# A RetNet and HGRN2 mixer step on one core: two spreads by TensorE go through DRAM, W_v sums move into the ramp, x sums move to VectorE, and some thirty positions in a hand-written order change

## The chip, the cores and the metric

The kernel runs on one core of one Trainium2 chip. The metric is device time in microseconds (us), the median of three runs of the whole program. Engine names are those of the profile: PE is TensorE, DVE is VectorE, ACT is ScalarE, POOL is GpSimd, SP is SyncE (which here only issues DMA).

## What is computed

One layer of a hybrid decoder, in fp32, for a prompt of 2048 tokens and for 8 new tokens ("decode rows") with their own states:

```python
h = rmsnorm(x, norm_g)
p = h @ w_in                              # 1024 -> 8 groups of 512
rq, rk, rv, rg, hq, hf, hi, hgate = split(p, 8)
o_ret, s_ret = chunked_decay_recurrence(rotary(rq), rotary(rk) * dk**-0.5, rv, log_gamma, s0)
o_hg,  s_hg  = chunked_decay_recurrence(silu(hq), (1 - lb) * sigmoid(-hf), hi, logf, s0)
o = concat(head_rmsnorm(o_ret) * silu(rg), head_rmsnorm(o_hg) * silu(hgate))
y = rmsnorm(x + o @ w_out, final_norm_g)
```

`rmsnorm` divides each token by its root mean square ("1/rms" below). Outputs are y for both sets of tokens and four new states.

## The kernel before

**Products.** Each fp32 operand is split into a high and a low part (ACT makes the high part, DVE subtracts it, L233, L272, L713), and a product is three matmuls, high by high, high by low, low by high. Big products are done in 2 x 2 blocks with seven block products in place of eight (Strassen-Winograd); the operands are sums of blocks, called T1 to T4 on one side and S1 to S4 on the other, beside plain blocks (A11, A12, A22, B11, B21, B22).

**Stages.** A *ramp* computes the values (retention and HGRN) of the first two token groups with plain products `pv` (L465), while loads come in; it begins with small warm-up matmuls `wu` (L200, L203) and holds the decode rows' value product `pvd` (L556). Then come units u = -6 to -1, the values of the other six groups; u = 0 to 23, the projections, three to a head group, with the HGRN steps in units 0, 3, 6, ... and the retention steps in units 2, 5, 8, ...; u = 24 to 31, the output projection. Each unit is seven slots long; a slot is one block product, twelve matmuls of 128 x 512 (`aV`, `eG`, `bR` and so on, L872).

**Order.** PE's program order is written out. For the other engines too the order is fixed: `at(pos, f)` puts a step on a heap at a position in slots (unit u starts at 7u; the values' units lie at negative positions), and steps are emitted by position. Most positions come from the table `AT`. Each engine runs its instructions strictly in that order, so that an instruction that waits holds up all behind it. SBUF tiles come from small rings: twelve temporary buffers, handed on in first-in, first-out order (`t_get`, `t_done`, L251, L267), and a few rings of named tiles. A DMA into a buffer waits for the buffer's last reader.

**The pieces that the change touches:**

- *x1's block rows.* x1 are the operands of the second half of the prompt. Its blocks are normalised by `x1_norm` (L1349), which multiplies by a row of 1/rms, laid along the free axis and the same on all partitions. To make it, `x1_dg` (L1314) puts four columns of 1/rms on the diagonals of four 128 x 128 blocks on DVE, `x1_spread` (L1321) multiplies ones by these on PE (`prb`, L701), copies the result on ACT and stores it to `rb_dram` on POOL's queue; `x1_rb` (L1343) loads it eight times on SP.
- *The decode row of 1/rms.* `decode_dg` (L578) and `decode_spread` (L581) do the same for the eight decode rows (`dgd`, `prsd`, `rbd`), and DVE then scales the decode tokens into `xz` (L586).
- *The W_v operands in the ramp.* `wv_subs` (L509) forms T1 to T4 of the value weights on DVE in place, `wv_parts` (L516) splits them, per k (0 to 3, each with k + 4). Those of k = 2, 3 end in the first unit (u = -6, position -42).
- *x sums.* `blocks_sums` (L424, operations L434) forms T1, T2, T3, T4 of the token blocks for the groups 6 and 7, in two halves each; two of these four are on DVE and two on POOL. Results are stored to `x_dram`; the next load waits for such stores.
- *Decode products.* `dec_mm` (L770, `pdp`, L778) multiplies the rows of W_in of a unit by `xz` on PE; for u = 3, 6, 9 it stands at `mm0`. It reads the freshly loaded weight blocks (`r3A`, `r3S`, loaded by `w_load`, L737).
- *Weight splits* (`w_split`, L757, ops L271 on ACT and L272 on DVE) make S1, S2, A12 and so on of the next unit's weights; *operand swaps* replace a low and high part of x1 or W_out (L709, L713); *rotation* `qr` (L967, L968, L716); *scores* `par` (L1140) and `pah`, `plh` (L1223, L1241, L1275, L1284), with the HGRN steps `kh`, `qth` (L1188, L1191) ahead of them; *transposes* `potr`, `poth` of the gated outputs and their gating `gtr`, `gth` (L1101, L1103).

Of the kernel before, what the change touches and what calls it, by code (L numbers as in the profile page):

```python
# [19 lines left out]
P = 128  # L20
# [28 lines left out]
def spooled(u):  # L49
# [10 lines left out]
          'load': 18.0,  # L60
# [10 lines left out]
 'ret': {'load': 12.0,  # L71
# [4 lines left out]
         'o0': 15.5,  # L76
         'st1': 15.7,
         'o1': 17.1,
         'last': 17.6,
         't0': 19.01,  # L80
         't1': 21.7},
# [6 lines left out]
       'sS1': -1.4,  # L88
# [3 lines left out]
       'sA12': 1.4,  # L92
       'sS3': 2.4,
       'sA22': 3.05},
 're': {'A11': -3.4, 'S1': -2.4, 'S2': -1.4, 'S4': -0.4, 'A12': 0.6, 'S3': 1.6, 'A22': 2.6},
 'dec': {'mm': -1.97, 'mm0': -3.42, 'copy': -0.9, 'copy0': -2.4, 'sel': 0.7},
# [10 lines left out]
          'B22': (8.9, 8.95, 9.2, 9.75),  # L107
          'B21': (9.45, 9.85, 10.0, 10.3),
          'T3': (11.3, 11.3, 11.8, 11.8),
          'T4': (14.2, 14.2, 14.7, 14.7)},  # L110
# [4 lines left out]
           'lB21': 6.4,  # L115
           'lT3': 8.4,
           'lT4': 12.2,
           'B11': (3.0, 3.0, 3.5, 3.5),
# [3 lines left out]
           'B21': (9.45, 9.85, 10.0, 10.3),  # L122
# [21 lines left out]
 'dhs': (-5.0, -2.2, -2.2, -1.5)}  # L144
# [5 lines left out]
def step_kernel(ctx, tc, a, out):  # L150
# [22 lines left out]
    vd_dram = dr.tile([2, NB, GW], F32, tag="vd_dram", name="vd_dram")  # L173
    v_dram = [
# [172 lines left out]

    spread_to = {}

# [74 lines left out]
    def blocks_sums(i, n):  # L424
# [8 lines left out]
        def less(o, x, y):  # L433
            (dve if (i, n) in ((6, 0), (7, 1)) else pool).tensor_tensor(o, x, y, op=ALU.subtract)  # L434
# [35 lines left out]
    def tok_load0(i, k0, cuts=1):  # L470
        r = x0r[i, k0] = t_get([P, 2, 256], f"x0r{i}{k0}")
        for n in range(0, 2, 2 // cuts):
            kk = slice(n, n + 2 // cuts)
            sp.dma_start(r[:, kk], a["x_t"][V_ORDER[i], :, k0 + kk.start : k0 + kk.stop])
# [101 lines left out]
    dgd = vq.tile([NB, NB], F32, tag="dgd", name="dgd")  # L576

    def decode_dg():  # L578
        dve.tensor_scalar(dgd, ident[:NB, :NB], rsd[:, 1:2], None, op0=ALU.mult)

    def decode_spread():  # L581
        pt = ps_tr.tile([P, NB], F32, tag="tr", name="prsd")
        pe.matmul(pt, ones[:NB, :], dgd, start=True, stop=True)
        rb = vq.tile([P, NB], F32, tag="rbd", name="rbd")
        act.activation(rb, pt, AF.Copy)
        dve.tensor_tensor(  # L586
            xz[:, : 32 * KT].rearrange("p (k b) -> p k b", b=32)[:, :, :NB], xs,
            rb.unsqueeze(1).to_broadcast([P, KT, NB]), op=ALU.mult,
        )
# [11 lines left out]
    tok_load0(0, 0, 2)  # L601
    wv_load(0, 2)
    act.activation(lb[:, 0:1], zero, AF.Sigmoid)
    tok_load0(0, 4)
    wv_load(4, 2)
    for k in (0, 4):
        x_split0(0, k)
        wv_split(k)
    wv_load(1)
    wv_load(5)  # L610
    for k in (1, 5):
        x_split0(0, k)
        wv_split(k)
    tok_load0(0, 2)
# [12 lines left out]
    sp.dma_start(pk, a["pack"])  # L627
    stats(1)
    decode_inputs()
    for k in range(KT):  # L630
        x_split0(1, k)
    pv0 = {(c, ty): bank([P, GW], f"pv0{c}{ty}") for c in range(2) for ty in range(2)}
# [5 lines left out]
    for m, k in enumerate((0, 4, 1, 5, 2, 6, 3, 7)):  # L638
        decode_values(m, k)
    first, second = ("T1", "T2"), ("T3", "T4")  # L640
# [9 lines left out]
    with tc.manual_schedule(engines=ORDERED):  # L650
        stats_load(2)
        for c in range(2):
            for ty in range(2):
                plain_out(0, c, ty, pv0[c, ty])
        wv_subs(0, first + second)
        wv_parts(0, first + second)
        tok_load(2)
        ps = plain_next(0, 1)
        stats_sum(2, True)
        stats_load(3)  # L660
        wv_subs(1, first + second)
        wv_parts(1, first + second)
        tok_load(3)
        plain_out(1, 0, 1, ps)
        stats_sum(3, True)
        spread_dg(2)
# [4 lines left out]
        wv_subs(2, first[:1])  # L671
        wv_subs(3, first[:1])
# [4 lines left out]
        wv_parts(2, first[:1])  # L677
        wv_parts(3, first[:1])
        tok_norm(2, 1)
        tok_sums(2, 0)  # L680
        s_split(2, "S1")
        plain_out(1, 0, 0, ps)
        wv_subs(2, second[:1])
        wv_subs(3, second[:1])
        wv_subs(2, first[1:])
# [1231 lines left out]
```

## Time and profile before

| | us |
|---|---|
| median of 3 runs (lowest, highest) | 1006.27 (1005.38, 1006.46) |
| the profiled execution | 1006.96 |
| its span, first to last instruction | 1005.2 |
| busy: PE, PE weight load | 987.3, 822.0 |
| busy: DVE, ACT, POOL | 783.6, 574.6, 256.2 |
| bytes moved | 244.56 MB, 243 GB/s |

Busy times are sums of instruction durations with overlaps counted once. Matmuls are pipelined: a 128 x 512 matmul lasts 0.39 us in a row, but the next starts 0.23 us after it, so that what a matmul costs is read from the difference of starts. DVE's operations overlap a little as well. A timeline row gives start, duration, engine, line of the kernel, operation, out<-in, the shape, and behind it in brackets the idle time before it with what ended it. Rows of a source line give shortest, median and longest duration in nanoseconds and the first and last start. A waits row gives total, count and longest wait. "issue" is time in which an engine waited for nothing that the profile shows.

### The profile page before, as it was taken

What the parts mean: (1) busy time and instruction counts of PE and PEld (TensorE: products, weight loads), DVE (VectorE), ACT (ScalarE), POOL (GpSimd) and SP (SyncE); (2) the same over time, 40 slices, a digit from 0 to 9 for tenths busy, and PEclk for the clock granted to TensorE, in tenths of its full rate; (3) what the DMA queues carried; (4) which work ended last, traced back from release to release, by engine and by line L of the source; (5) the groups of instructions that cost most, each with busy time, mean ns of one, the idle gap of its engine ahead of it and who ended that gap; (6) DMA issues with size and microseconds to landing.
All of it is one profiled execution on the core that took longest, in us unless ns stands there. A gap on an engine that the chain in (4) does not pass through costs nothing.

```text
span 1005.2 us, 22979 instructions
## 1 busy us (share of the span) xinstructions
PE 987.3 (98%) x8824; PEld 822.0 (82%) x8824; DVE 783.6 (78%) x1361; ACT 574.6 (57%) x1348; POOL 256.2 (25%) x404
## 2 busy tenths in 40 slices
PE   9999999999999999999999999999999999999997
PEld 8788877888888888888788788888888878877885
DVE  6797696879869978887898766877866799767774
ACT  7754523847655664765885555456467577524332
POOL 0211271112332433232012222222222602313121
PEclk9999999999999999999999999999999999999999
DMA  9746659838958878785985993993996396674522
GB/s 332 242 150 238 222 189 357 313 114 298 305 171 306 304 239 287 279 253 184 348 261 175 303 321 119 304 335 109 309 370 218 111 406 228 238 263 155 206 88 83
DMA packets 121340, 244.56 MB, mean 243 GB/s; under 512 B 12128, under 2 KB 52448, under 8 KB 118544
## 3 DMA queue, kind: packets, MB, share of 16 engines
q1 hardware_dynamic: 97968, 164.68, 48.9%
q0 software_dynamic: 22976, 78.17, 21.0%
q8 instruction: 69, 1.13, 0.5%
q14 instruction: 39, 0.32, 0.1%
q10 hardware_dynamic: 288, 0.27, 0.1%
HBM read 155.97 MB, written 90.24 MB: 245 GB/s over the span
## 4 chain that ended last, share of the span: by engine, by line
PE 84%; DVE 7%; ACT 4%; issue 2%; DMA 1%; POOL 1%; POOLq 0%; SPq 0%; DVEq 0%; ACTq 0%
PE aH L872 9%; PE aG L872 8%; PE aO L872 7%; PE aR L872 7%; PE aV L872 5%; PE eG L872 4%; PE eH L872 4%; PE pv L465 4%; PE eO L872 4%; PE eR L872 3%; PE eV L872 2%; PE bH L872 2%; PE bG L872 2%; PE bO L872 2%; PE bR L872 2%
## 5 line engine op out<-in xcount | busy, mean ns | idle before, releaser
L1639 ACT ACTIVATE yj<-xro 128x512 f32<-128x512 f32 x24 | 15.2, 632 | 66.9 <-DVE xro L716 33.2
L1202 ACT ACTIVATE qh<-kh 128x1024 f32<-128x1024 f32 x24 | 25.5, 1061 | 47.3 <-DVE kh L1188 47.3
L1188 DVE TENSOR_TENSOR kh<-kh,fph 128x512 f32<-128x512 f32 x48 | 32.9, 686 | 11.4 <-PE plh L1223 10.5
L949 ACT ACTIVATE sg<-g 128x512 f32<-128x512 f32 x26 | 16.4, 631 | 36.3 <-DVE g L716 35.8
L1082 ACT ACTIVATE obh<-poh 128x128 f32<-128x128 f32 x64 | 16.9, 287 | 32.5 <-PE poh L1078 32.5
L1191 DVE TENSOR_TENSOR qth<-qth,fph 128x512 f32<-128x512 f32 x48 | 32.9, 685 | 0.0
L1082 ACT ACTIVATE obr<-por 128x128 f32<-128x128 f32 x64 | 16.8, 276 | 27.3 <-PE por L1078 27.3
L716 DVE TENSOR_TENSOR xro<-aO,xro 128x512 f32<-128x512 f32 x33 | 22.5, 685 | 8.1 <-PE aO L872 7.8
L1106 POOL DMA_DIRECT2D o_dram<-gth x16 | 12.4, 773 | 62.6 <-DVE gth L1103 23.4
L1090 ACT ACTIVATE obh<-poh,orsh 128x128 f32<-128x128 f32 x64 | 18.2, 366 | 16.5 <-POOL orsh L229 16.4
L336 POOL TENSOR_TENSOR ms<-ms 128x2 f32<-128x2 f32 x8 | 3.0, 370 | 95.4 <-ACT xn L332 95.4
L956 POOL DMA_DIRECT2D g_dram<-g x31 | 16.9, 548 | 39.0 <-DVE g L952 33.9
L1090 ACT ACTIVATE obr<-por,orsr 128x128 f32<-128x128 f32 x64 | 18.2, 368 | 14.6 <-POOL orsr L229 14.6
L228 POOL TENSOR_SCALAR orsh<-omsh 128x4 f32<-128x4 f32 x16 | 4.9, 308 | 84.1 <-ACT obh L1082 83.8
L902 ACT ACTIVATE vo<-aV 128x512 f32<-128x512 f32 x12 | 7.1, 592 | 32.4 <-PE aV L872 32.1
L1069 DVE SCALAR_TENSOR_TENSOR sth<-sth,fph,puh 128x128 f32<-128x128 f32 x48 | 16.7, 347 | 11.0 <-PE poh L1078 8.5
L1106 POOL DMA_DIRECT2D o_dram<-gtr x16 | 12.5, 782 | 46.3 <-DVE g L716 14.0
L1076 PE MATMUL poh<-vh,A 128*128 128x128 f32 x128 | 24.0, 274 | 0.0
L1076 PE MATMUL por<-vr,A 128*128 128x128 f32 x128 | 24.0, 274 | 0.0
L228 POOL TENSOR_SCALAR orsr<-omsr,pk 128x4 f32<-128x4 f32 x16 | 7.6, 474 | 57.5 <-ACT obr L1082 57.5
L1653 DVE SCALAR_TENSOR_TENSOR xro<-xro,yms,fg 128x1024 f32<-128x1024 f32 (+1 forms) x16 | 19.9, 1245 | 3.0 <-POOL yms L1650 3.0
L1078 PE MATMUL poh<-sth,qth 128*128 128x128 f32 x112 | 21.7, 275 | 0.0
(1712 smaller groups left out, 3760.0 us busy)
## 6 DMA issues: line engine op xcount, KB each, us to landing
xn<-in_x_prompt SPq DMA_DIRECT2D x32, 256.0 KB, 4.7
v_dram<-vo SPq DMA_DIRECT2D x32, 256.0 KB, 3.4
xro<-in_x_prompt SPq DMA_DIRECT2D x16, 512.0 KB, 5.8
g_dram<-g POOLq DMA_DIRECT2D x31, 256.0 KB, 5.6
out_y_prompt<-xro POOLq DMA_DIRECT2D x15, 512.0 KB, 3.4
xr<-in_x_t SPq DMA_DIRECT2D x12, 512.0 KB, 5.7
vh<-v_dram SPq DMA_DIRECT2D x16, 256.0 KB, 8.0
gth<-g_dram SPq DMA_DIRECT2D x16, 256.0 KB, 6.8
```

Of the source, the lines that this page charges most:

```text
L465: pe.matmul(ps, xx, ww, start=(first and n == 0), stop=(last and n == 2))
L716: dve.tensor_tensor(o, x, y, op=ALU.add)
L872: pe.matmul(ps, w[i], x[j], start=(first and k == 0 and m == 0), stop=(k == 3 and m == 2), skip_group_check=True,)
L1076: pe.matmul(po[:, j], s_ctx["A"][:, c], box["v"][g][:, j], start=True, stop=src is None)
L1078: pe.matmul(po[:, j], qcol(c), src, start=False, stop=True)
L1082: act.activation(ob[:, j], po[:, j], AF.Square, accum_out=ms[:, j : j + 1])
L1090: act.activation(ob[:, j], po[:, j], AF.Copy, scale=rs[:, j : j + 1])
L1106: after(AT["gate"]["tr"], lambda: pool.dma_start(o_dram[c0 : c0 + 4, ty, :, h].rearrange("c p t -> p c t"), gt.rearrange("p (c t) -> p c t ...
L1188: dve.tensor_tensor(kv[:, :, 0, :], kv[:, :, 0, :], two[:, :, 1:2].to_broadcast([P, nb, b]), op=ALU.mult)
L1191: dve.tensor_tensor(qv[:, :, 1, :], qv[:, :, 1, :], two[:, :, 0:1].to_broadcast([P, nb, b]), op=ALU.mult)
L1202: act.activation(kept_k, k, AF.Copy)
L1653: dve.scalar_tensor_tensor(x[:, cc], x[:, cc], ms[:, 0:1], fg[:, cc], op0=ALU.mult, op1=ALU.mult)
```

## The change

1. *x1's block rows* leave PE. `x1_dg`, `x1_spread`, `blk_spread` and `rb_dram` are gone. `rows_store` stores four columns of 1/rms to `rs_dram` from POOL's queue, at positions -24.2 and -20.2, and `x1_rb` loads from it with a broadcast over partitions.
2. *The decode row* goes the same way: `decode_dg` is a store to `rsd_dram` on POOL's queue at -31.4, `decode_load` a broadcast load on SP at -24.4; the multiplication into `xz` stays at -15.4.
3. *Ramp.* The first x loads are cut into halves, and the decode tokens' part of `pack` is loaded first. The decode value product for k = 0, 4, 1, 5 stands in the middle of the first group's products, and the W_v sums and parts of k = 0, 1 behind it; those of k = 2, 3, and three steps of group 2, move from the first unit into the ramp. Warm-up: 25 pairs in place of 17.
4. *x sums* all run on DVE.
5. *Positions.* Some thirty entries of `AT` move, by 0.15 to 1.5 slots; u > 20 gets tables of its own for the retention and HGRN steps (`retL`, `hgrnL`), and u = 3 gets two HGRN steps half a slot earlier.

The diff, cut to its core:

```diff
- 'ret': {'load': 12.0,
+ 'ret': {'load': 12.5,
...
-          'o0': 15.5,
+          'o0': 15.0,
...
-          't0': 19.01,
-          't1': 21.7},
+          't0': 19.51,
+          't1': 23.2},
...
-       'sS1': -1.4,
+       'sS1': -1.25,
...
-       'sA12': 1.4,
-       'sS3': 2.4,
-       'sA22': 3.05},
+       'sA12': 1.9,
+       'sS3': 2.25,
+       'sA22': 3.3},
...
- 'dec': {'mm': -1.97, 'mm0': -3.42, 'copy': -0.9, 'copy0': -2.4, 'sel': 0.7},
+ 'dec': {'mm': -1.97, 'mm0': -3.92, 'copy': -0.9, 'copy0': -2.4, 'sel': 0.7},
...
- 'wu': 17,
- 'wop': (140.0, 1.8, 2.0, 2.6),
+ 'wu': 25,
+ 'wop': (140.0, 2.133, 2.1, 2.6),
...
- 'fin': 0.75,
+ 'fin': 1.0,
...
+    def rows_store(c):
+        pool.dma_start(rs_dram[c : c + 4].rearrange("c p -> p c"), rs_all[:, c : c + 4])
...
-            (dve if (i, n) in ((6, 0), (7, 1)) else pool).tensor_tensor(o, x, y, op=ALU.subtract)
+            dve.tensor_tensor(o, x, y, op=ALU.subtract)
...
     def decode_dg():
-        dve.tensor_scalar(dgd, ident[:NB, :NB], rsd[:, 1:2], None, op0=ALU.mult)
-
-    def decode_spread():
-        pt = ps_tr.tile([P, NB], F32, tag="tr", name="prsd")
-        pe.matmul(pt, ones[:NB, :], dgd, start=True, stop=True)
-        rb = vq.tile([P, NB], F32, tag="rbd", name="rbd")
-        act.activation(rb, pt, AF.Copy)
+        pool.dma_start(rsd_dram, rsd[:, 1:2])
+
+    def decode_load():
+        rbd = vq.tile([P, NB], F32, tag="rbd", name="rbd")
+        sp.dma_start(rbd, rsd_dram.partition_broadcast(P))
+        return rbd
...
+        if kk == 1:
+            decode_inputs()
+            for m, k in enumerate((0, 4, 1, 5)):
+                decode_values(m, k)
+            for k in range(2):
+                wv_subs(k, first + second)
+                wv_parts(k, first + second)
+    for m, k in enumerate((2, 6, 3, 7)):
+        decode_values(m + 4, k)
...
-    def blk_spread(blk, dg, dst):
-        pt = ps_tr.tile([P, 4, P], F32, tag="tr", name=f"prb{blk}")
-        for j in range(4):
-            pe.matmul(pt[:, j], ones, dg[:, j], start=True, stop=True)
-        act.activation(dst, pt.rearrange("p a b -> p (a b)"), AF.Copy)
...
-        sp.dma_start(xd["rb"], rb_dram[n])
+        c = 8 + 4 * TB[n]
+        sp.dma_start(xd["rb"].rearrange("p (c t) -> p c t", c=4), rs_dram[c : c + 4].partition_broadcast(P))
...
-    at(-21 + 3.6, decode_dg)
-    at(-21 + 5.6, decode_spread)
+
+    at(-35 + 3.6, decode_dg)
+    for n in range(2):
+        at(-24.2 + 4 * n, lambda n=n: rows_store(8 + 4 * n))
+    box_d = {}
+    at(-28 + 3.6, lambda: box_d.update(t=decode_load()))
+    at(-21 + 5.6, lambda: decode_spread(box_d["t"]))
```

How it moves instructions is shown at three places, all on DVE. (Line numbers are those of each kernel, names end in the program's own numbers.)

In the ramp, before: `wvT1l`, `B12l`, `wvT4l`, `wvT3l` are the low parts of plain W_v blocks, here of k = 2 (and 6) and then k = 3 (and 7); PE reads them in the first group's products.

```order
L233 TENSOR_TENSOR wvT1l_169<-wvr20_232,wvT1h_168 128x512
L233 TENSOR_TENSOR B12l1_185<-wvr21_233,B12h1_183 128x512
L233 TENSOR_TENSOR wvT4l_177<-wvr60_236,wvT4h_176 128x512
L233 TENSOR_TENSOR wvT3l_175<-wvr61_237,wvT3h_174 128x512
L233 TENSOR_TENSOR wvT1l_169<-wvr3_256,wvT1h_168 128x512
L233 TENSOR_TENSOR B12l1_185<-wvr3_256,B12h1_183 128x512
L233 TENSOR_TENSOR wvT4l_177<-wvr7_258,wvT4h_176 128x512
L233 TENSOR_TENSOR wvT3l_175<-wvr7_258,wvT3h_174 128x512
```

The same place now, from k = 6 on:

```order
L270 TENSOR_TENSOR wvT3l_184<-wvr61_248,wvT3h_183 128x512
L553 TENSOR_TENSOR wvr0_199<-wvr0_199 128x512
L553 TENSOR_TENSOR wvr0_199<-wvr4_205,wvr0_199 128x512
L553 TENSOR_TENSOR wvr1_222<-wvr1_222 128x512
L553 TENSOR_TENSOR wvr4_205<-wvr4_205,wvr0_199 128x512
L270 TENSOR_TENSOR wvT2l_180<-wvr0_199,wvT2h_179 128x512
L553 TENSOR_TENSOR wvr4_205<-wvr4_205 128x512
L270 TENSOR_TENSOR wvB22l_182<-wvr4_205,wvB22h_181 128x512
L270 TENSOR_TENSOR wvT1l_178<-wvr3_267,wvT1h_177 128x512
L270 TENSOR_TENSOR B12l1_194<-wvr3_267,B12h1_192 128x512
L270 TENSOR_TENSOR T3l_188<-wvr0_199,T3h_187 128x512
L270 TENSOR_TENSOR wvT4l_186<-wvr7_269,wvT4h_185 128x512
```

Seven operations on the sums of k = 0, 1 stand between k = 2's parts and k = 3's, and an eighth among k = 3's.

At u = 21, before: `gtr121` is a gating of the retention steps, `kh13`, `qth13` and `plh131` belong to the HGRN scores, `w23...` are splits of later weights.

```order
L1103 TENSOR_TENSOR gtr121_9278<-potr121_9475,gtr121_9278 128x512
L272 TENSOR_TENSOR w23S4_9481<-r23S4_9448,w23S4_9481 128x512
L952 SCALAR_TENSOR_TENSOR g2222_9216<-g2222_9216,pk_148,sg2222_9461 128x512
L272 TENSOR_TENSOR w23A12_9493<-big_1757,w23A12_9493 128x512
L1188 TENSOR_TENSOR kh13_9066<-kh13_9066,fph13_9400 128x128x4
L1191 TENSOR_TENSOR qth13_9177<-qth13_9177,fph13_9400 128x128x4
L1229 COPY_PREDICATED fh13_8871<-lmask_149,plh131_9507 128x64x2
```

The same place now, some rows further down as well:

```order
L309 TENSOR_TENSOR w23S4_9466<-r23S4_9436,w23S4_9466 128x512
L994 SCALAR_TENSOR_TENSOR g2222_9202<-g2222_9202,pk_157,sg2222_9460 128x512
L1230 TENSOR_TENSOR kh13_9058<-kh13_9058,fph13_9404 128x128x4
L1233 TENSOR_TENSOR qth13_9188<-qth13_9188,fph13_9404 128x128x4
L309 TENSOR_TENSOR w23A12_9559<-big_1768,w23A12_9559 128x512
L1271 COPY_PREDICATED fh13_8854<-lmask_158,plh131_9488 128x64x2
L1271 COPY_PREDICATED fh13_8854<-lmask_158,plh131_9488 128x32x4
L1589 TENSOR_TENSOR draw_164<-draw_164,dsq_8958 128x64
L1590 TENSOR_TENSOR draw_164<-draw_164,dg_163 128x64
L1145 TENSOR_TENSOR gtr121_9264<-potr121_9576,gtr121_9264 128x512
L309 TENSOR_TENSOR w23S3_9582<-r23S3_9212,w23S3_9582 128x512
```

`gtr121` has moved behind the scores' copies, right ahead of the split of w23's S3, and `kh13`, `qth13` now stand ahead of w23's A12.

At the end of u = 23, before: `woB21l` is the low part of an operand of the output projection, made in two halves; `qr13` is the rotated query that `par` reads; `xro0` takes up the output projection's first results.

```order
L713 TENSOR_TENSOR woB21l_9815<-woB21l_9815,woB21h_9814 128x1024
L272 TENSOR_TENSOR w24A22_9980<-r24A22_9595,w24A22_9980 128x512
L713 TENSOR_TENSOR woB21l_9815<-woB21l_9815,woB21h_9814 128x1024
L967 TENSOR_TENSOR qr13_9505<-qr13_9505,ctab1_5965 128x512
L968 TENSOR_TENSOR sw2321_9959<-sw2321_9959,stab1_5967 128x512
L716 TENSOR_TENSOR qr13_9505<-qr13_9505,sw2321_9959 128x512
L716 TENSOR_TENSOR xro0_9823<-aO240_9852,xro0_9823 128x512
L716 TENSOR_TENSOR xro0_9823<-eO241_9875,xro0_9823 128x512
```

The same place now:

```order
L753 TENSOR_TENSOR woB21l_9841<-woB21l_9841,woB21h_9840 128x1024
L309 TENSOR_TENSOR w24A22_9971<-r24A22_9585,w24A22_9971 128x512
L1009 TENSOR_TENSOR qr13_9485<-qr13_9485,ctab1_5957 128x512
L1010 TENSOR_TENSOR sw2321_9949<-sw2321_9949,stab1_5959 128x512
L756 TENSOR_TENSOR qr13_9485<-qr13_9485,sw2321_9949 128x512
L756 TENSOR_TENSOR xro0_9809<-aO240_9843,xro0_9809 128x512
L753 TENSOR_TENSOR woB21l_9841<-woB21l_9841,woB21h_9840 128x1024
L756 TENSOR_TENSOR xro0_9809<-eO241_9866,xro0_9809 128x512
```

The second half of `woB21l` has moved from ahead of the rotation to behind the first `xro0`.

More of the change, by code (lines that the diff above doesn't have):

```diff
@@ L468, in step_kernel, with tok_load0 @@
     x0_left = {(i, k): [0, 1] for i in range(2) for k in range(4)}
[L470 to L474, printed above, removed]
+    def tok_load0(i, k0, ks=(0, 1)):
+        if (i, k0) not in x0r:
+            x0r[i, k0] = t_get([P, 2, 256], f"x0r{i}{k0}")
+        kk = slice(ks[0], ks[-1] + 1)
+        sp.dma_start(x0r[i, k0][:, kk], a["x_t"][V_ORDER[i], :, k0 + kk.start : k0 + kk.stop])
     def x_split0(i, k):
@@ L626, in step_kernel @@
         tok_load0(1, k)
-    sp.dma_start(pk, a["pack"])
+    for x in (slice(0, xs_at.start), slice(xs_at.stop, PACK_W)):
+        sp.dma_start(pk[:, x], a["pack"][:, x])
     stats(1)
-    decode_inputs()
     for k in range(KT):
         x_split0(1, k)
+    first, second = ("T1", "T2"), ("T3", "T4")
     pv0 = {(c, ty): bank([P, GW], f"pv0{c}{ty}") for c in range(2) for ty in range(2)}
```

151 lines of the change are left out of this document (81 added, 70 removed).

## The prediction

> **What bounds the kernel now.** I read the page first (busy times, chain), then the waits of PE, then the timelines of PE and DVE around each wait. Engine rows and chain:
>
> ```profile
> span 1005.2 us, 22979 instructions
> PE 987.3 (98%) x8824; PEld 822.0 (82%) x8824; DVE 783.6 (78%) x1361; ACT 574.6 (57%) x1348; POOL 256.2 (25%) x404
> PE 84%; DVE 7%; ACT 4%; issue 2%; DMA 1%; POOL 1%; POOLq 0%; SPq 0%; DVEq 0%; ACTq 0%
> ```
>
> PE is busy 98% of the span, and the chain that ends last is mostly PE behind PE. So time falls only where PE gets less work or waits less. All of PE's waits (total, times, longest):
>
> ```profile
> PE plh L1284 <- DVE qth L1191: 2.2, 2, 1.5
> PE plh L1223 <- issue: 2.0, 2, 1.0
> PE pah L1223 <- issue: 1.5, 1, 1.5
> PE wu L200 <- POOL ones L191: 1.1, 1, 1.1
> PE aO L872 <- DVE xro L716: 0.9, 1, 0.9
> PE par L1140 <- DVE qr L716: 0.7, 1, 0.7
> PE poth L1101 <- DVE gth L1103: 0.6, 1, 0.6
> PE plh L1223 <- DVE qth L1191: 0.5, 2, 0.3
> PE aV L872 <- DVE vo L716: 0.4, 1, 0.4
> PE eH L872 <- DVE x1T1l L713: 0.4, 1, 0.4
> PE prs L363 <- DVE dg L356: 0.2, 1, 0.2
> ```
>
> They sum to 10.5 us: 1.1 before the first instruction, 3.5 of "issue", 5.9 behind DVE. Even a perfect order could save no more than these 9.4 and the PE work that the change deletes. The profiled execution took 1006.96 us, 1.8 around its span and 0.7 above the median of 1006.27; I make the sum in differences and put it to the median.
>
> **PE work removed.** The block rows of x1 are spread by `prb` twice (one for each block row), the decode row by `prsd` once:
>
> ```profile
> 205.46 0.40 PE L872 MATMUL aG<-x0T2h,w1S 128*128 128x512 f32 x1
> 205.69 1.05 PE L701 MATMUL prb<-dgx,ones 128*128 128x128 f32 x8
> 206.50 0.47 PE L872 MATMUL eG<-x0B22h,w1S 128*128 128x512 f32 x1
> 206.82 0.39 PE L872 MATMUL eG<-x0B22l,w1S 128*128 128x512 f32 x1
> ...
> 127.62 0.38 PE L583 MATMUL prsd<-dgd,ones 8*128 8x8 f32 x2
> 127.93 0.50 PE L872 MATMUL aV<-T3h,s5S 128*128 128x512 f32 x1
> ```
>
> Matmuls overlap, so starts are subtracted. A usual 128x512 step is 205.69 - 205.46 = 0.23. `prb` holds PE from 205.69 to 206.50, 0.81, and the step behind it is 0.32 instead of 0.23: 0.9. Twice: 1.8. `prsd` holds it 0.31, and with such longer steps on both sides some 0.5. Nothing replaces them on PE: **-2.3**, the term I am surest of.
>
> **PE work added.** The ramp's decode product `pvd` is cut into two groups, which adds one change between small and wide matmuls: +0.1, by the step behind `prb`. The warm-up gets 16 more small matmuls:
>
> ```profile
> 5.92 0.48 PE L203 MATMUL wu<-ones 128*32 128x8 f32 x34
> 6.33 0.49 PE L465 MATMUL pv<-wvT1h,x0B11h 128*128 128x512 f32 x1
> ```
>
> 34 of them take 6.33 - 5.92 = 0.41, so 16 take 0.2 if the operands are there at 6.33 and nothing if these come later. The halved first loads bring them no later. I take +0.1, between 0 and +0.2. The Trainium skill, "TensorE: Matmul & The Clock Gate", "Part 1: The HAM clock gate", speaks against this edit: the clock rises after about 3.4 us of sustained work, so by it the eight added pairs buy nothing. No row here shows a start with another number of pairs, so it stays open which holds; the difference is the 0.1.
>
> **DVE order behind PE's waits.** The next rows are DVE's at u=23 (the wait of `par`), u=21 (`plh`) and u=23's transposes (`poth`):
>
> ```profile
> 836.93 1.22 DVE L713 TENSOR_TENSOR woB21l<-woB21l,woB21h 128x1024 fp32r<-128x1024 f32 x1
> 839.39 0.69 DVE L716 TENSOR_TENSOR qr<-qr,sw 128x512 f32<-128x512 f32 x1
> ...
> 804.58 0.69 DVE L272 TENSOR_TENSOR w23S<-r23S,w23S 128x512 fp32r<-128x512 f32 x1 [0.54 <-ACT w23S L271]
> ...
> 848.78 0.69 DVE L272 TENSOR_TENSOR w25S<-r25S,w25S 128x512 fp32r<-128x512 f32 x1 [0.71 <-ACT w25S L271]
> ```
>
> At u=23 the second half of woB21l (1.22) stands ahead of the rotation that `par` waits for; now it goes behind the rotation and the first xro. The 0.7 goes; woB21l is late next, by about two such operations, with the product that reads it still a group of `par` away: -0.7. At u=25's weights DVE sits idle 0.71 for ACT with gth queued behind it; now gth stands ahead: -0.6. At u=21 DVE is full, and its idle 0.54 ahead of w23S is the only air: one gtr (0.69, a 128x512 operation) is moved there from the full part, and kh, qth go ahead of a w23A split. I take 1.0 of that 1.5 as gone (between 0.5 and 1.5), and 0.3 of the 0.7 that is left of the same row at u=9 (0 to 0.7), where two operations are exchanged in the same manner. These four give **-2.6**.
>
> **x sums.** Eight sums go from POOL to DVE. Of the old place:
>
> ```profile
> 131.41 2.02 DVE L399 TENSOR_TENSOR S<-xr,S 128x512 f32<-128x512 f32 x1
> ...
> 131.56 1.31 POOL L434 TENSOR_TENSOR bT<-bs61B,xr 128x512 f32<-128x512 f32 x1
> ```
>
> DVE gains 8 x 0.69 = 5.5 of work. But its own operation beside a POOL sum takes 2.02 where the shape takes 0.69, 1.3 lost; were each of the eight to cost as much, DVE would win back 10.6. So DVE's net lies between +4.2 and -5.1; I take zero. The chain of loads and stores to the next unit's vo gets shorter (1.31 on POOL against 0.69, eight times), and the wait of aV goes: **-0.4**. With no winnings DVE would be 4.2 late, which PE's own lead must cover.
>
> **Ramp.** The W_v sums of k=0, 1 now stand ahead of the parts of k=3, which the ramp's last products read:
>
> ```profile
> L233 DVE TENSOR_TENSOR wvT3l<-wvr,wvT3h x4: 684/684/693, 9.3 to 23.0; 128x512 fp32r<-128x512 f32 x4
> 27.33 0.39 PE L465 MATMUL pv<-wvT3l,x0B21h 128*128 128x512 f32 x1
> 28.56 3.64 PE L556 MATMUL pvd<-wvr,pk 128*32 128x512 f32 x32
> ```
>
> The last wvT3l ends at 23.7; PE wants it at 27.33, and half of `pvd` (1.8) now comes before that. So the lead is 27.33 - 23.7 + 1.8 = 5.4, and eight operations of at most 0.69 (5.5) stand in front, some of them in time that DVE now spends waiting for loads: it just holds. Zero, up to +1 if ACT, which makes the high parts that these subtract, trails too. The later parts of k=2, 3 have the plain products as cover.
>
> **Loads.** The x1 rows now come from `rs_dram` by a broadcast load, the same 256 KB in the same places:
>
> ```profile
> L1345 SPq DMA_DIRECT2D rb<-rb_dram x7: 326/332/522, 232.8 to 413.9; - x7
> DMA to landing us min/median/max: 3.5/5.8/10.1
> ...
> L1349 DVE SCALAR_TENSOR_TENSOR x1B<-x1B,g_in,rb x11: 743/745/747, 252.8 to 429.5; 128x512 f32<-128x512 f32 x11
> ```
>
> The first is issued at 232.8 and used at 252.8, 20 us for at most 10.1 now: hidden at double that. The stores of 4-byte elements and the decode row's way through DRAM have no row here; the nearest are these landings, 3.5 to 10.1. The rows are stored over a hundred us ahead of 232.8, and the decode row's load is issued nine slots (of twelve 0.23 us steps, so 25 us) ahead of its use, so even the slowest landing twice over is covered; I take nothing. Queued behind the stores on POOL are x stores and sums of squares, behind the load on SP the token loads; both are wanted slots later. With the old spreads, DVE loses two `dgx` and a `dgd`, ACT three evacuations and POOL two stores; none of them ends a wait of PE in the table, so they bring nothing. The other moves (retention and HGRN loads, gate steps, swaps, w_out loads) shift work by half a slot where no wait stands in the rows; I cost them together at **+0.5** of new waits (0 to 2), the last row of the waits (`prs`) growing among them.
>
> Instruction fetch can move with any shift of PE's stream:
>
> ```profile
> 297.24 0.26 PE L1223 MATMUL pah<-qth,kh 128*32 128x16 f32 x8 [1.54 <-issue]
> ...
> q8 instruction: 1, 0.02, 2.9%
> ```
>
> PE stands 1.54 us with all operands there, and the DMA view of 294.3 to 297.3 has one instruction packet in it. PE's stream loses 36 instructions (weight loads counted) and gains 32, so the fetches fall in nearly the same places: 0, with 1.5 either way. The Trainium skill, "Runtime: NRT & Kernel Launch", "Instruction fetch mechanics", holds a refill to be mostly hidden; by it this would be 0 either way. The row differs, and the row decides.
>
> **Sum:** -2.3 + 0.2 - 2.6 - 0.4 + 0.5 = -4.6 us, so **1001.7 us** against the median.
>
> **Rivals.** A: only the PE work goes. PE is in order and DVE supplies it all the way, so waits that are taken away turn up a few products later: -2.3 + 0.2 + 0.5 = -1.6, 1004.7. For it: DVE full around u=21. Against it: at u=23 and u=25 DVE has room right behind.
>
> B: more goes. A shorter stall upstream also clears the rest of DVE's waits (5.9 - 3.0 = 2.9): -7.5, 998.8. For it: aO, eH and the rest of plh are each under 1 us. Against it: no edit touches aO's chain.
>
> C, slower: the decode rows. `pdp` of u=3, 6, 9 is moved half a slot (1.4 us) earlier, and a PE that waits there holds up everything.
>
> ```profile
> L740 SPq DMA_DIRECT2D r3A<-in_w_in x3: 328/328/328, 214.0 to 225.3; - x3
> ...
> L778 PE MATMUL pdp<-r3A,xz x24: 272/273/297, 230.7 to 231.5; 128*32 128x128 f32 x24
> ...
> r3A<-in_w_in SPq DMA_DIRECT2D x2, 256.0 KB, 4.2
> vh<-v_dram SPq DMA_DIRECT2D x2, 256.0 KB, 7.7
> ```
>
> The last row block is issued at 225.3, lands 4.2 later at 229.5, and would be wanted at 229.3. If it is issued no earlier and takes 7.7, as the load next in its queue, PE waits 3.7, three times: -4.6 + 11.1 = +6.5, 1012.8. It decides from a landing 1.5 us past need. Against it: the order gives this load a buffer that DVE frees sooner than the g store did.
>
> D: the rows through DRAM aren't there in time at 252.8 or for the decode row; PE would lose by C's price. Little speaks for it.
>
> **Chances.** About 0.2% (2 us) is what a measurement can tell from no change: bounds 1004.3 and 1008.3. Forecast 0.62 (nearly all faster), A 0.19 (0.14 of it within 0.2%, 0.05 faster), B 0.08 (faster), C 0.08 (0.07 slower), D 0.03 (0.02 slower). So faster 0.74, same 0.17, slower 0.09. The range runs from just below B, 998.3, to A and its 0.6 of unknown waits, 1005.3; it leaves out C, D and some tails.
>
> **What would show it.** Right: no `prb` or `prsd` rows and PE's busy time down by 2; no waits of `par`, `poth`, `aV`; `plh` behind qth under 1.2 in all; DVE at 0.69 where 2.02 stood; issue waits still near 3.5. Wrong: a new wait of PE over 1 us behind DVE in u=18 to 26 (A), at `pdp` behind a DMA (C), or in the ramp behind wvT1l.

## The result, and the profile after

The changed kernel takes **1022.14 us** (median of six runs, 1018.52 to 1023.64) where the kernel before takes 1006.66 (six runs, 1005.38 to 1008.22): a ratio of means of **1.0149, 95% interval 1.0127 to 1.017** (ratios are of means, times are medians, here and below). It is slower by some 15 us, and the forecast of 1001.7 and its range failed. The profiled execution took 1018.52 us, with a span of 1016.7; it is the fastest of the six.

The page of the changed kernel, engine row and chain, then the row of PE's busy tenths and of its granted clock over the 40 slices of the span (25.4 us each):

```profile
PE 989.1 (97%) x8822; PEld 821.8 (81%) x8822; DVE 781.9 (77%) x1366; ACT 574.7 (57%) x1345; POOL 247.3 (24%) x397
...
PE   9999959999999999999999999999999989999997
...
PEclk9999979999999999999999999999999999999999
...
PE 80%; DVE 7%; DMA 5%; ACT 4%; issue 2%; POOL 0%; SPq 0%; POOLq 0%; DVEq 0%; ACTq 0%
```

One slice, the sixth (127 to 152 us), falls to 5 for PE and 7 for its clock. DMA, 1% of the chain before, is 5% now. That places it in the values' stage, before u = 0. PE's waits, the longest first:

```profile
PE prs L402 <- DVE dg L395: 8.9, 1, 8.9
PE plh L1326 <- DVE qth L1233: 2.7, 1, 2.7
PE aV L914 <- DVE xz L626: 2.6, 1, 2.6
PE plh L1265 <- issue: 1.4, 1, 1.4
...
PE aV L914 <- ACT vo L634: 0.9, 1, 0.9
```

The wait of `prs` is the row that was last and smallest before (0.2). Where it happens, PE's timeline:

```profile
131.06 0.39 PE L914 MATMUL aV<-T3h,s5S 128*128 128x512 f32 x1
134.03 0.69 PE L914 MATMUL aV<-wvT1h,x0B11h 128*128 128x512 f32 x1 [2.58 <-DVE xz L626]
134.52 0.63 PE L914 MATMUL aV<-wvT1l,x0B11h 128*128 128x512 f32 x1
134.95 0.63 PE L914 MATMUL aV<-wvT1h,x0B11l 128*128 128x512 f32 x1
...
140.97 0.39 PE L914 MATMUL eV<-wvT2h,s6S 128*128 128x512 f32 x1
150.22 1.19 PE L402 MATMUL prs<-dg,ones 128*128 128x128 f32 x4 [8.86 <-DVE dg L395]
```

The starts show a second price: behind the stall a step takes 134.95 - 134.52 = 0.43 where 0.23 is usual. POOL's timeline shows what the new stores do:

```profile
105.77 0.85 POOL L386 DMA_DIRECT2D rs_dram<-rs_all  x1
117.09 0.72 POOL L451 DMA_DIRECT2D b_dram<-xr  x1 [10.47 <-issue]
...
131.34 0.78 POOL L386 DMA_DIRECT2D rs_dram<-rs_all  x1 [5.18 <-issue]
...
134.09 0.80 POOL L469 DMA_DIRECT2D x_dram<-bT  x1
144.03 0.73 POOL L469 DMA_DIRECT2D x_dram<-bT  x1 [9.15 <-issue]
```

Behind the first of the two new stores of 1/rms (2 KB) POOL's next DMA comes after a gap of 10.47 us; behind the second one more is issued, and then there is a gap of 9.15. The view of the DMA issues gives the two stores 11.7 us to landing, where a block of 512 KB from the same queue takes 5.6:

```profile
b_dram<-xr POOLq DMA_DIRECT2D x2, 512.0 KB, 5.6
...
rs_dram<-rs_all POOLq DMA_DIRECT2D x2, 2.0 KB, 11.7
```

POOL's queue isn't the only one held. In the DMA view of 107.5 to 116.5, the row of q1, SP's queue, gives packets, MB and the share of 16 engines' time that the packets took. In the first row, after the change, it moves under a third of the bytes of the second, before, and its packets take more of the time:

```profile
q1 hardware_dynamic: 234, 0.45, 83.5%
q1 hardware_dynamic: 811, 1.49, 53.2%
```

Behind the stores stand those of the x blocks on POOL's queue. DVE and ACT, in order, stand before operations that need what slow transfers still hold, DVE behind a store of SP's queue and ACT behind one of POOL's:

```profile
144.73 0.69 DVE L473 TENSOR_TENSOR bT<-bs61B,xr 128x512 f32<-128x512 f32 x1 [10.71 <-DMA v_dram<-vo]
...
146.98 0.60 ACT L944 ACTIVATE vo<-aV 128x512 f32<-128x512 f32 x1 [17.76 <-DMA x_dram<-bT]
```

DVE's `dg`, which `prs` needs, is queued behind the sums of bs61. The chain that ends at `prs` (start, duration) runs through transfers of SP's queue, loads of xn and a store of v_dram, which before land after 4.4 and 2.4 to 2.8 us:

```profile
117.52 7.85 DMA xn<-in_x_prompt
...
132.51 12.12 DMA v_dram<-vo
```

Starts of stages in the profiled runs, from PE's timelines, us ("ramp" is the first product, "values" u = -6):

```
              before    after   rows on PE   late stores   last version
ramp            6.33     6.30      6.26         7.53          6.92
values         54.89    55.76     55.39        57.68         56.54
u = 0         175.55   190.60    174.65       176.89        175.80
u = 2         218.07   231.29    217.22       217.59        216.49
u = 3         243.07   256.62    244.21       242.89        241.61
u = 9         410.53   425.64    415.68       411.89        412.88
u = 12        493.03   507.10    497.24       493.40        494.41
u = 15        575.12   588.48    577.96       574.93        575.78
u = 24        819.23   833.04    825.67       821.21        819.70
u = 25        848.00   860.79    853.41       848.94        847.72
u = 28        918.79   930.36    922.97       918.51        917.31
PE's end      997.92  1009.48   1002.10       997.63        996.48
```

From before to after: +0.9 in the ramp, +14.2 in the values' stage, and -3.5 in all the rest, 11.6 in the profiled runs. Where the slower runs of the changed kernel lose some 4 us more, no profile shows.

### The profile page after: what moved, and what is told of

The parts are those of the page before. It is cut to its first block, busy times and chain, and to the rows that moved or that the text cites. A ratio compares the mean times of both kernels' runs of the same rounds, so it can differ in the third digit from the quotient of the medians.

```text
span 1016.7 us, 22964 instructions
## 1 busy us (share of the span) xinstructions
PE 989.1 (97%) x8822; PEld 821.8 (81%) x8822; DVE 781.9 (77%) x1366; ACT 574.7 (57%) x1345; POOL 247.3 (24%) x397
## 4 chain that ended last, share of the span: by engine, by line
PE 80%; DVE 7%; DMA 5%; ACT 4%; issue 2%; POOL 0%; SPq 0%; POOLq 0%; DVEq 0%; ACTq 0%
PE aG L914 8%; PE aO L914 8%; PE aH L914 7%; PE aR L914 7%; PE aV L914 6%; PE eG L914 4%; PE eR L914 4%; PE eO L914 4%; PE eH L914 3%; PE eV L914 2%; PE bG L914 2%; PE bO L914 2%; PE bH L914 2%; PE bR L914 2%; DMA xn<-in_x_prompt 2%
## 5 line engine op out<-in xcount | busy, mean ns | idle before, releaser
L1662 ACT ACTIVATE yj<-xro 128x512 f32<-128x512 f32 x29 | 18.3, 632 | 74.1 <-DVE xro L756 40.4
L1148 POOL DMA_DIRECT2D o_dram<-gtr x16 | 12.4, 777 | 59.5 <-DVE gtr L1145 17.9
L1111 DVE SCALAR_TENSOR_TENSOR sth<-sth,fph,puh 128x128 f32<-128x128 f32 x48 | 16.6, 347 | 10.1 <-PE poh L1120 7.5
L369 ACT ACTIVATE xn<-xn 128x512 f32<-128x512 f32 x32 | 19.9, 624 | 6.1 <-DMA xn<-in_x_prompt 6.1
L1120 PE MATMUL por<-str,qr 128*128 128x128 f32 x112 | 21.9, 277 | 0.4 <-DVE str L1109 0.4
L1118 PEld LDWEIGHTS por<-vr,A 128*128 128x128 f32 x128 | 20.3, 191 | 1.3
```

What stands on the lines that cost most here:

```text
L369: act.activation(r, r, AF.Square, accum_out=ms[:, 2 * h + j : 2 * h + j + 1])
L1118: pe.matmul(po[:, j], s_ctx["A"][:, c], box["v"][g][:, j], start=True, stop=src is None)
L1120: pe.matmul(po[:, j], qcol(c), src, start=False, stop=True)
L1148: after(AT["gate"]["tr"], lambda: pool.dma_start(o_dram[c0 : c0 + 4, ty, :, h].rearrange("c p t -> p c t"), gt.rearrange("p (c t) -> p c t ...
```

## The experiments

**Theories.** T1: a store of 512 elements of 4 bytes holds POOL's DMA queue some 10 us, and what stands behind it comes late. T2: the x sums on DVE did it. T3: the small writes slow all DMA, whichever queue has them. Later C (decode products too early), F (instruction fetch), L and G (the wait of `plh`) came in.

### The stores alone, added to the kernel before

```diff
+    def rows_store(c):
+        pool.dma_start(rs_dram[c : c + 4].rearrange("c p -> p c"), rs_all[:, c : c + 4])
...
+    for n in range(2):
+        at(-24.2 + 4 * n, lambda n=n: rows_store(8 + 4 * n))
```

> The kernel before with nothing but the two stores of 4-byte elements added at positions -24.2 and -20.2 (nobody reads them; x1's rows still come from TensorE). T1: the stalls appear here too, 1016 to 1023, with issue waits of 9 to 10 us on POOL behind each store. T2: 1006 to 1007.5, since the x sums stay where they were. T3: 1016 to 1023.

1022.81 us, ratio 1.0159 (1.0143 to 1.0174). Two stores that nobody reads make the kernel before as slow as the changed one. PE's longest wait, the landing, and POOL's issue wait of this run:

```profile
PE prs L367 <- DVE dg L360: 11.7, 3, 11.2
...
rs_dram<-rs_all POOLq DMA_DIRECT2D x2, 2.0 KB, 12.0
...
POOL x_dram L434 <- issue: 10.6, 3, 9.5
```

T2 is refuted: the x sums are where they were. T1 and T3 both expected this time.

### The same bytes in 128 pieces

Against the kernel with the stores alone:

```diff
-    rs_dram = dr.tile([T // P, P], F32, tag="rs_dram", name="rs_dram")
+    rs_dram = dr.tile([T // GW, P, 4], F32, tag="rs_dram", name="rs_dram")
...
-        pool.dma_start(rs_dram[c : c + 4].rearrange("c p -> p c"), rs_all[:, c : c + 4])
+        pool.dma_start(rs_dram[c // 4], rs_all[:, c : c + 4])
```

> The kernel before with two stores of the same 2 KB each at -24.2 and -20.2 as in the run with the two stores alone, but laid out so that each partition writes its four values side by side (16 bytes in one piece, 128 pieces in place of 512 of 4 bytes). Nobody reads them. If the hold on POOL's queue goes by the number of pieces: 3 to 4 us a store, issue waits of 1 to 3 us, time 1007 to 1011. If it goes by the bytes or by the store itself: 1019 to 1024 as with the 4-byte pieces.

1006.24, ratio 1.0 (0.999 to 1.0011): nothing, and under both expected ranges. DMA issues and POOL's timeline:

```profile
rs_dram<-rs_all POOLq DMA_DIRECT2D x2, 2.0 KB, 4.6
...
106.02 0.63 POOL L350 DMA_DIRECT2D rs_dram<-rs_all  x1
106.65 0.77 POOL L416 DMA_DIRECT2D b_dram<-xr  x1
```

The next store is issued at once. The bytes, the queue and the place are the same; 512 pieces of 4 bytes became 128 of 16. The price is that of how the store is cut up, and it isn't in proportion to the number of pieces: landing takes 4.6 us, and there is no hold at all.

### x1's rows on TensorE again

```diff
-        at(-24.2 + 4 * n, lambda n=n: rows_store(8 + 4 * n))
...
+        at(9.2 + n, lambda n=n: x1_dg(n))
+        at(10.6 + n, lambda n=n: x1_spread(n))
```

> The changed kernel with its part 1 undone: x1's block rows are spread by TensorE and stored as 256 KB again, no store of 4-byte elements; all other parts stay. Theory T1 (each store of 512 elements of 4 bytes holds POOL's DMA queue some 10 us, and the x blocks stored behind it come late): the two stalls of the values' stage vanish, time 1004 to 1006 (1006.5, +0.9 in the ramp, -3.5 in the later stages of the traces, of which 1.8 is given back). Rival T2 (the x sums that moved to DVE cause the stalls): 1018 to 1024 as the changed kernel. Rival T3 (the small writes slow all DMA, whichever queue has them): as T1.

1011.27 (1009.36 to 1013.69), ratio 1.005 (1.0035 to 1.0065). The stall is gone, 11 us with it: u = 0 starts at 174.65. But the time is 5 us over the number of T1 and T3 (T2's is 7 over it), so a second cause was left. Some of its waits:

```profile
PE plh L1332 <- DVE qth L1239: 2.5, 1, 2.5
PE eR L920 <- issue: 1.8, 1, 1.8
...
PE pdp L824 <- DMA r3A<-in_w_in: 1.3, 1, 1.3
```

### The stores later

```diff
-        at(-24.2 + 4 * n, lambda n=n: rows_store(8 + 4 * n))
+        at(11.3 + 4.6 * n, lambda n=n: rows_store(8 + 4 * n))
```

> The changed kernel with only the two stores of 4-byte elements moved from positions -24.2 and -20.2 to 11.3 and 15.9, where POOL's queue has nothing to issue for some 28 us. T1: the stores are as slow as before (11 to 12 us to landing), nothing stands behind them, no stall in the values' stage: 1002.5 to 1004.5. T2: 1018 to 1024, stalls unchanged. T3: the stall moves to units 1 and 2, where weights are loaded: 1006 to 1018.

The values' stage runs free (u = 0 at 174.70), but nine runs lie between 1004.43 and 1016.62, median 1014.39, ratio 1.0048 (1.0019 to 1.0076): over T1's number, inside T3's. I had put the second store badly: position 15.9 comes behind w2's stores, and POOL reaches it at 229.40, in a full stretch. The stall went with it. POOL's and PE's timelines, and the DMA view of 236.5 to 242:

```profile
229.40 0.77 POOL L386 DMA_DIRECT2D rs_dram<-rs_all  x1 [5.08 <-issue]
...
237.05 0.54 POOL L802 DMA_DIRECT2D w_dram<-w2S  x1 [6.03 <-issue]
```

```profile
231.86 0.84 PE L1265 MATMUL plh<-qth,kh 128*32 128x16 f32 x41
235.66 0.40 PE L1265 MATMUL plh<-qth,kh 128*32 128x16 f32 x21 [2.95 <-issue]
...
q8 instruction: 1, 0.02, 5.7%
```

Here PE waits 2.95 us, until 235.66, with no operand missing. What it waits for isn't shown: the DMA view of 232.5 to 236 has no packet of instructions. The one in the view of 236.5 to 242 fills 5.7% of 16 engines over 5.5 us, so 5.0 us of one engine; the packet in the prediction's rows, 2.9% of 16 over 3 us, took 1.4. So a store in small pieces holds up more than its own queue: T3 has a share.

### The stores on SP's queue

```diff
-        pool.dma_start(rs_dram[c : c + 4].rearrange("c p -> p c"), rs_all[:, c : c + 4])
+        sp.dma_start(rs_dram[c : c + 4].rearrange("c p -> p c"), rs_all[:, c : c + 4])
```

> The changed kernel with the two stores of 4-byte elements issued from SP's queue in place of POOL's, at the same positions. T1: POOL's x stores are issued without waits; whether SP's queue is held in the same way (sums-of-squares and x loads stand behind) is open: 1002.5 to 1005 if it isn't, 1010 to 1022 if it is. T2: 1018 to 1024. T3: 1015 to 1023, since the small writes are the same.

1013.01, ratio 1.0068 (1.0053 to 1.0082), under T3's range and inside the one that T1 gave for a held SP queue. The values' stage takes 124.1 us, against 134.8 in the changed kernel and 119.3 with the rows on PE. Of the 15.5 us, 10.7 go when the pieces leave POOL's queue, and 4.8, a third, stay when SP issues them: POOL's next store still waits, though it has none of them ahead of it, and the chain to PE's longest wait of the stage (`aV`, 2.8) runs through loads of xn:

```profile
POOL x_dram L452 <- issue: 8.4, 1, 8.4
...
116.36 11.07 DMA xn<-in_x_prompt
```

Since the chain of the changed kernel runs through SP's transfers too, the 10.7 aren't shown to be POOL's wait to issue alone. Both T1's hold and T3's slow transfers are there; their shares stay open.

### Both stores in the gap of POOL's queue

```diff
-        at(-24.2 + 4 * n, lambda n=n: rows_store(8 + 4 * n))
+        at(11.3 + 0.1 * n, lambda n=n: rows_store(8 + 4 * n))
```

> The changed kernel with the two stores of 4-byte elements at 11.3 and 11.4 and nothing else. T1: the stall of the values' stage is gone and none takes its place in u = 1 to 3, so the time is that of the kernel with the rows on TensorE (1011.3) less its 1.8 of TensorE work: 1008 to 1010, and the runs no longer spread over 12 us as with the store at 229 us. C: waits of pdp behind r3A and r6A stay. T2 (DVE sums): 1018 to 1024.

1006.6 (twelve runs, 1004.59 to 1009.52), ratio 1.0006 (0.9993 to 1.0018): moving two DMAs by some 32 and 36 slots takes 15.5 us off. The stores are as slow there (11.46 us pass on POOL before the second can be issued), but no stall of PE follows. The time is 1.4 us under the expected range, and in its profile no `pdp` waits; yet it only equals the kernel before. With the decode products put back as well:

```diff
- 'dec': {'mm': -1.97, 'mm0': -3.92, 'copy': -0.9, 'copy0': -2.4, 'sel': 0.7},
+ 'dec': {'mm': -1.97, 'mm0': -3.42, 'copy': -0.9, 'copy0': -2.4, 'sel': 0.7},
```

> The changed kernel with the two stores of 4-byte elements side by side at positions 11.3 and 11.4 (POOL's queue has nothing else to issue from 187 to 214 us in the run with late rows) and with the decode products of u = 3, 6, 9 back at -3.42. Theory T1 (a store holds POOL's queue some 11 us): no stall behind the stores. Theory C (decode rows are wanted before they land): the waits of pdp behind r3A, r6A, r7A (1.3 to 1.7, 0.6 to 0.9, 0.2 to 0.5 in the runs so far) go, and the time is 1.5 to 4 below the next kernel's, 1003.5 to 1007. Rival F (what is left over the forecast is instruction fetch, whose waits fall anew in every variant): the time is the next kernel's, give or take 2.

1007.0, ratio 1.001 (0.9995 to 1.0024), the same within the intervals. Theory C as a cost of the early products isn't shown by these times: in the profiles `pdp` waits for r3A in four kernels with the early position (1.3 to 1.7 us), not in three others with it (the changed kernel, the late stores, and the sums on POOL below), and not in this one. The load's lead is that thin.

### Parts alone

The change with every position of the kernel before (stores at 11.3; three of some 30 entries):

```diff
-       'sS1': -1.25,
+       'sS1': -1.4,
...
-       'sA12': 1.9,
...
+       'sA12': 1.4,
...
- 'wu': 25,
...
+ 'wu': 17,
```

> Parts 1 to 4 of the change (stores of 4-byte elements at 11.3 and 11.4), with every position of the kernel before: no decode rows early, no other moves, warm-up of 17 pairs. If the positions (part 5) cost what is left: 1003 to 1005.5 (1006.5 less 2.3 of TensorE work, with 0.5 to 0.9 given back in the ramp). If parts 3 or 4 cost it (W_v sums in the ramp, x sums on DVE): 1007 to 1011.

1011.26, ratio 1.0051 (1.0036 to 1.0065). Part 1 alone in the kernel before (stores at 11.3):

```diff
-        at(9.2 + n, lambda n=n: x1_dg(n))
-        at(10.6 + n, lambda n=n: x1_spread(n))
+        at(11.3 + 0.1 * n, lambda n=n: rows_store(8 + 4 * n))
```

> The kernel before with part 1 alone: x1's block rows through DRAM, the two stores at 11.3 and 11.4. T1 with the TensorE work sized as forecast: 1006.5 - 1.8 = 1004.7, between 1004 and 1005.5. Rival F (fetch waits move with the 32 instructions that are gone): anything from 1003 to 1008 with the difference in issue waits.

1008.99 (1005.6 to 1012.45), ratio 1.0024 (1.0011 to 1.0038). Both miss, the first by 0.26 over its second range. The moved positions are worth 4.7 us to parts 1 to 4, against my reading; and taking 1.8 us of work off PE alone makes the kernel slower. A wait of `pdp` has appeared in both, with the products at their old place; of part 1 alone:

```profile
PE plh L1227 <- issue: 3.9, 2, 2.5
PE pdp L782 <- DMA big<-in_w_in: 2.1, 1, 2.1
```

In these orders the last row block of u = 3 still waits for a g store. With part 1 alone it is issued at 225.34, as before, and PE, ready at 230.35, goes on at 232.49, so it lands later: rival C's price, though no product was moved. Why it took longer wasn't settled. Behind the wait of 2.5 for "issue" the granted clock is 0.50 from 401.5 to 404.9; in the kernel before it stays at 1.00 from the ramp to PE's end. The x sums back on POOL for two halves (stores at 11.3):

```diff
-            dve.tensor_tensor(o, x, y, op=ALU.subtract)
+            (dve if (i, n) in ((6, 0), (7, 1)) else pool).tensor_tensor(o, x, y, op=ALU.subtract)
```

> The kernel with both stores at 11.3 and 11.4, with part 4 undone: the x sums of two of the four halves on POOL again. If moving them to DVE was worth the wait of aV (0.4) and some slack: 0.4 to 1.5 above the kernel with them on DVE, 1007 to 1008; the 2.02 of a DVE operation beside a POOL sum is back. T2 (the DVE sums cost time): lower than with them on DVE, 1004 to 1006.

1009.5, ratio 1.0037 (1.0022 to 1.0053), against 1006.6 with the sums on DVE and over both expected ranges. The slow operation is back, but the values' stage of its profiled run takes 119.25 us, as with the sums on DVE (119.21), and no wait of aV behind DVE's vo has come back:

```profile
132.42 2.00 DVE L438 TENSOR_TENSOR S<-xr,S 128x512 f32<-128x512 f32 x1
```

So the 2.9 us aren't lost at the sums. In the profiles this run has waits of `pdp` for r6A (1.0) and r7A (0.3) that the run with late stores lacks; how the sums lead there stays open.

### The wait of plh at u = 23

This is the wait that the prediction calls that of u=21: the scores belong to unit 21's steps and run during u = 23. In the seven kernels so far with the new positions `plh` waits 2.5 to 3.4 us behind DVE, where I had forecast 0.5. DVE's timeline with late stores, and PE's:

```profile
810.95 0.69 DVE L756 TENSOR_TENSOR kr<-eR,kr 128x512 f32<-128x512 f32 x1
813.36 0.69 DVE L768 TENSOR_TENSOR r24S<-r24S,r24A 128x512 f32<-128x512 f32 x1 [1.73 <-DMA r24A<-o_dram]
813.97 0.69 DVE L1230 TENSOR_TENSOR kh<-kh,fph 128x512 f32<-128x512 f32 x1
814.57 0.69 DVE L1233 TENSOR_TENSOR qth<-qth,fph 128x512 f32<-128x512 f32 x1
...
815.40 0.65 PE L1326 MATMUL plh<-qth,kh 128*32 128x64 f32 x32 [2.87 <-DVE qth L1233]
```

DVE is not full: it stands 1.73 us before a sum for unit 24, whose load hasn't landed. The wait also has a second price: in the 3.4 us behind it the granted clock (last column but two) is 0.50, here and in four more of the seven profiles:

```profile
816.00:819.40 3.40, 3.40 (x13) 2.72 (x9) 3.40 (x7) 3.20 (x8) 0.00 (x0) 0.50 0.99 408
```

By the steps behind the stall in the values' stage (0.43 for 0.23) that costs up to 1.6 us more, an estimate. The test moves those sums behind kh and qth:

```diff
- 'w24': (-5.6, -2.4, -1.9, -1.45, -0.45),
+ 'w24': (-5.6, -1.28, -1.2, -1.27, -0.45),
```

> The kernel with both stores at 11.3 and 11.4 (parts 1 to 5 else), with the sums S1, S2, S3 of unit 24's operands moved on DVE from ahead of the last kh and qth of u = 21 to behind them. Theory L (the wait of plh behind qth, 2.7 to 3.4 us in all variants with the new positions, is DVE standing in front of a load of r24A that hasn't landed, not DVE being full): that wait falls from 2.9 to under 1.5, time 1.5 to 2.5 lower, 1004 to 1005.2. Rival G (DVE is full there, as the forecast had it): the wait only changes by the two operations moved, 1.2, and comes back at the first product of u = 24: 1006 to 1007.

1005.72, ratio 0.9989 (0.9977 to 1.0002). In this kernel S2 is formed ahead of S3, which changes an operand that both use, so unit 24 computes something else; the operations and their times are the same. The time lies between the ranges of L and G; the wait fell as L had it, though a new one of 1.0 took part of it:

```profile
PE pkh L1081 <- ACT A L1336: 1.0, 1, 1.0
PE plh L1326 <- DVE qth L1233: 1.0, 1, 1.0
```

From u = 23 to u = 24 it takes 27.40 us, against 28.88 with late stores and 26.67 before, and the clock stays at 1.00 there. DVE's idle before the sum is gone, and the wait doesn't come back at the first product of u = 24, so rival G is refuted.

### What the runs spoke for, together

```diff
- 'dec': {'mm': -1.97, 'mm0': -3.92, 'copy': -0.9, 'copy0': -2.4, 'sel': 0.7},
+ 'dec': {'mm': -1.97, 'mm0': -3.42, 'copy': -0.9, 'copy0': -2.4, 'sel': 0.7},
...
- 'w24': (-5.6, -2.4, -1.9, -1.45, -0.45),
+ 'w24': (-5.6, -1.28, -1.27, -1.26, -0.45),
...
-        at(-24.2 + 4 * n, lambda n=n: rows_store(8 + 4 * n))
+        at(11.3 + 0.1 * n, lambda n=n: rows_store(8 + 4 * n))
```

> The changed kernel with what the runs spoke against undone: both stores of 4-byte elements at 11.3 and 11.4, the decode products of u = 3, 6, 9 back at -3.42, and unit 24's sums S1, S3, S2 (in this order) behind the last kh and qth of u = 21. Theory L and C: 1.4 to 2.2 under the kernel with late stores at u = 23, no waits of pdp, so 1003.5 to 1005.5 and faster than the kernel before by 0.1 to 0.3%. If what is left is instruction fetch and load timing that every variant meets anew (F): 1005 to 1007.5, no difference from before.

**1005.29** (eleven runs, 1004.31 to 1008.28), ratio **0.9989 (0.998 to 0.9998)**: clearly faster than the changed kernel, and under the kernel before by 0.1%, less than the 0.2% that the prediction took for measurable. The time lies in the ranges of both theories, and `pdp` still waits 0.4 for r7A, so F isn't ruled out. From u = 23 to u = 24 it takes 26.06 us, 0.6 less than before. Two of its longest waits, of "issue" and of a vo:

```profile
PE plh L1265 <- issue: 2.8, 2, 2.6
...
PE aV L914 <- ACT vo L634: 1.1, 1, 1.1
```

## Why the prediction was wrong, point by point

1. **The step that failed is the one on loads.** For the stores of 4-byte elements the prediction had no row, took the nearest, landings of 3.5 to 10.1 us of block loads, found them covered and wrote "I take nothing"; of the x stores and sums of squares behind them on POOL it said that they are "wanted slots later". The landing, 11.0 and 12.4 us, was indeed covered: no reader waits for `rs_dram`. What had no term is what such a store does to the DMAs beside and behind it until it lands. POOL's next DMA comes 10.5 us later (b_dram's store 11 us later than before), and loads of xn and a store of v_dram on SP's queue take 7.9 and 12.1 us in the chain to `prs`. So a term put at nothing was 14.2 us in the values' stage. I had asked when the row is needed and not what its store holds up meanwhile. Named rivals were of the wrong place: D priced a late row, C a late weight. The stores alone give +16 (shown by adding them), their removal -11, their move -15.5.

2. **PE work removed** was right as work. From u = 1 to u = 2, where `prb` stood, the changed kernel, the late stores and the last version all take 1.8 us less than before, the kernel with the rows on PE 0.05 more (forecast 1.8). The values' stage, which holds `prsd`, shortens by 1.4 in the kernels without the stall and with the new positions; the forecast was 0.5 and 0.4 for aV's wait. As time it didn't show by itself: part 1 alone is 2.4 slower than before, and its profile has a wait of `pdp`, longer waits of "issue" and a stretch at half the clock that the kernel before hasn't.

3. **par, poth.** From u = 24 to u = 26 the changed kernel gains 1.34 (forecast 0.7 + 0.6), and `par` and `poth` are out of the waits. aO's wait, for which I saw no edit, went as well: 0.9 from u = 27 to u = 28. That piece of rival B happened.

4. **plh at u = 21** went the other way: I took DVE's order for the limit and forecast -1.0, measured is +1.2 (2.7 against 1.5). The moves did bring DVE ahead: in the run with late stores the kr operation ahead of the wait begins at 810.95, 1.0 us earlier than before. But the next operation in the queue then stood 1.73 us before a load. Before, the same sum begins at 812.76, 0.81 behind the start of kr, where its neighbours follow at 0.6, so the load may have been close to the limit there already. I didn't ask what DVE would wait for next, nor what a wait of this length does to the clock.

5. **The ramp** cost 0.5 to 1.6 where I had said 0, up to 1, but by another way: PE waits for the evacuation vo of a plain product, which ACT has queued behind operations that wait for DVE, which waits for the last sums of squares. wvT1l was in time. The first product's start itself differs by 1.2 us between kernels whose code ahead of it is the same (6.30 and 7.53).

6. **Instruction fetch**: the waits of "issue" sum to 2.6 in the changed kernel and to 2.2 to 6.5 over the variants, where I had 3.5 with 1.5 either way: right for the change, too narrow for its variants.

7. **x sums.** aV's wait behind DVE's vo went, as forecast. The sums' move was worth nothing to the stage's length (119.21 and 119.25), so neither of the bounds of DVE's net showed; with no winnings at all DVE would have been 5.5 late, not the 4.2 that I wrote.

8. Of the remaining rivals, A's shape came true once the stall was removed: with late stores the gains of 2 and 3 (some 5 us) are met by waits of plh, vo and "issue" and by 3.4 us at half the clock, and the sum is zero. I had given this 0.19.

## What to carry to other kernels

A DMA has two prices: when its data lands, and what it holds up meanwhile on its own and on other queues; ask both, and look at how a store is cut up, not at its bytes alone. Before giving an engine air, check that what it will do in that air has its operands: an in-order engine that is early only waits at the next load. Of moves that each remove a few tenths, test each against the same base: here one of five parts cost 15.

## What the runs showed of the hardware

- A 2 KB store from 128 partitions in 512 pieces of 4 bytes lands after 11 to 14 us, and with it comes a gap of 9 to 13 in POOL's DMA issues; in 128 pieces of 16 bytes it lands after 4.6, with no gap. The Trainium skill, "DMA: Bandwidth & Descriptors", "Specifications", puts transfers under 512 bytes below line rate, with a read-modify-write. The pieces of both stores lie under that limit, so that rule alone doesn't tell them apart. Whether the count of the pieces, their size or the order of their addresses does wasn't separated: all changed together.
- Such a store slows transfers on other queues too: from 107.5 to 116.5 SP's queue moved 0.45 MB in the changed kernel and 1.49 before, and a fetch of instructions took 5.0 us beside one in the run with the second store at 229.40 and 5.2 in the run with both stores in the gap (5.4% of 16 engines over 196 to 202), against 1.4 in the prediction's rows.
- After an idle of 2.6 us (131.45 to 134.03) PE's steps take 0.43 instead of 0.23 until 137.51, eight steps and some 1.6 us more. The rows of the changed kernel in windows of 1 us, the granted clock in the last column but two:

```profile
133.00:134.00 1.00, 0.00 (x0) 0.00 (x0) 1.00 (x3) 0.00 (x0) 0.92 (x2) 1.00 1.08 147
134.00:135.00 1.00, 0.97 (x3) 0.81 (x4) 0.02 (x1) 0.00 (x0) 0.89 (x2) 0.55 0.80 169
...
138.00:139.00 1.00, 1.00 (x6) 0.83 (x5) 0.00 (x0) 0.00 (x0) 0.00 (x0) 1.00 0.79 90
```

  The clock is still 1.00 while PE idles and falls to 0.5 just as work resumes, for 3.4 us. The Trainium skill, "TensorE: Matmul & The Clock Gate", "Part 1: The HAM clock gate", has the gate close after an idle window of about 3.4 us and open after as long a busy one. The trace agrees with the second number; for the first, an idle of 2.6 us was enough here. The length of the idle alone doesn't decide: PE's wait of 2.6 for "issue" in the last version, until 402.30, left the clock at 1.00.
